# The low part of every eighth weight chunk of the MLPs made by an accumulating DMA

## The chip, the cores and the metric

The kernel runs on one core of one Trainium2 chip. The metric is the device time of one execution in microseconds (us), lower being better, as the median of repeated runs on one chip. Five engines work side by side on the core: TensorE (PE: matmuls, with the weight loads shown apart as PEld), VectorE (DVE), ScalarE (ACT), GpSimd (POOL), which here has had almost nothing to do, and SyncE (SP), which issues the large loads. Transfers from HBM are carried by 16 DMA engines.

## The reference, cut to what matters

The program is a trunk of two layers for 256 tokens of width 2048. Each layer is a mixer (attention and a delta rule in layer 0, dilated attention in layer 1) and an MLP of squared ReLU. Only the MLPs are touched by the change:

```python
D_MODEL, SEQ, DEPTH, D_FF = 2048, 256, 2, 8192

def squared_relu_mlp(h, w1, w2):          # h 256x2048, w1 2048x8192, w2 8192x2048, float32
    return jnp.square(jax.nn.relu(h @ w1)) @ w2

for l in range(DEPTH):
    x = x + mixer_l(rms_norm(x, ...))
    x = x + squared_relu_mlp(rms_norm(x, mlp_norm[l]), mlp_w1[l], mlp_w2[l])
```

## The kernel before, in words

Every large product goes through `dense`. It multiplies 256 tokens (two halves `h` of 128) with a stripe of a weight matrix that is 512 columns wide. The rows of the stripe are taken in chunks `kc` of 128, 16 chunks to a call in the MLPs, so a chunk is a tile of 128x512 float32, 256 KB. Two chunks arrive with one DMA that SP issues (`wload`, 512 KB, the tile whose name ends in `r`; four such buffers).

The product is formed from a high and a low part of each operand. ACT rounds the chunk to the type float32r (line 201, a CAST; tile `...h`, here called the high part). DVE subtracts that from the chunk (line 107 through the helper `tt`; tile `...l`, the low part). The activations were split in the same way earlier. PE then makes three matmuls for each of the two halves: high by high (line 206), high by low part of the weights (line 207), low by high part of the weights (line 208), six for each chunk, all summed in PSUM. High and low parts of the weights have six buffers each, so that ACT and DVE can be at most six chunks ahead of PE; `tc.high_priority(offset=AHEAD)` lets the scheduler place them early.

An MLP runs over four groups `g`. In each group four calls of `dense` make blocks of the hidden layer (names `m_0` to `m_3` in the profile, `b` from 0 to 3), and four calls multiply them with the second matrix (`n_0` to `n_3`). That is 2 layers x 4 groups x 8 calls x 16 chunks = 1024 chunks. After an `m` call ACT applies ReLU and the square (line 123, tiles `m_0r` and so on). `spread` then turns that block for the next product: 16 transposes on DVE (line 289, tile `m_0hT`), a CAST on ACT for its high part (line 314, `m_0hh`) and a subtraction on DVE for its low part (`m_0hl`). These steps are generators; `drip`, called once for each chunk, lets one step of them be recorded in turn, so they stand in ACT's and DVE's queues between the chunks of the next call. Each engine works through its own queue in order, and an instruction that waits holds up all behind it.

In the rows of the program's order below, `m0_0_2l15` is layer 0, group 0, third `m` call, low part of chunk 15; `p0` and `p1` are the sums of the two halves. The profile leaves layer, group and chunk out of a name. Waits name the engine or the DMA semaphore that is waited for.

Of the kernel before, what the change touches and what calls it, by code (L numbers as in the profile page):

```python
# [11 lines left out]
F32 = mybir.dt.float32  # L12
F32R = mybir.dt.float32r
I32 = mybir.dt.int32
AF = mybir.ActivationFunctionType
ALU = mybir.AluOpType
# [3 lines left out]
P = 128  # L20
# [67 lines left out]
def trunk(  # L88
# [5 lines left out]
    V, S, G, E = nc.vector, nc.scalar, nc.gpsimd, nc.tensor  # L94
# [11 lines left out]
    def tt(o, a, b, op):  # L106
        V.tensor_tensor(out=o, in0=a, in1=b, op=op)  # L107
# [13 lines left out]
    def act(o, a, f, scale=1.0, bias=0.0, accum=None):  # L121
        if accum is None:
            S.activation(out=o, in_=a, func=f, scale=scale, bias=bias)  # L123
        else:
            S.activation(out=o, in_=a, func=f, scale=scale, bias=bias, accum_out=accum)
# [45 lines left out]
    def wload(wsrc, k0, nm):  # L171
        raw = wp.tile([P, 2, 512], F32, tag="wr", name=f"{nm}r{k0}", bufs=4)
        off = 0
        for s in wsrc:
            m = s.shape[1]
            nc.sync.dma_start(raw[:, :, off:off + m], s[k0 * P:(k0 + 2) * P, :].rearrange("(c p) n -> p c n", p=P))
            off += m
        return raw
# [3 lines left out]
    def drip():  # L182

        step("gs"[tick[0] % 2])
        if tick[0] % 4 == 3:
            step("o")
        tick[0] += 1

    def dense(wsrc, stat, kcs, nm, pre=(), every=1):

        n = sum(s.shape[1] for s in wsrc)
        ps = [psd.tile([P, 512], F32, tag="d", name=f"{nm}p{h}") for h in range(NH)]
        first, last = kcs[0], kcs[-1]
        for j, kc in enumerate(kcs):
            if j % 2 == 0:
                raw = pre[j // 2] if j // 2 < len(pre) else wload(wsrc, kc, nm)
            w = raw[:, j % 2, :n]
            wh = wp.tile([P, 512], F32R, tag="wh", name=f"{nm}h{kc}")[:, :n]
            wl = wp.tile([P, 512], F32R, tag="wl", name=f"{nm}l{kc}")[:, :n]
            with tc.high_priority(offset=AHEAD):  # L200
                S.copy(wh, w)  # L201
                tt(wl, w, wh.bitcast(F32), ALU.subtract)
            for h in range(NH):
                sh, sl = stat(kc, h)
                o = ps[h][:, :n]
                E.matmul(o, lhsT=sh, rhs=wh, start=kc == first, stop=False)  # L206
                E.matmul(o, lhsT=sh, rhs=wl, start=False, stop=False)  # L207
                E.matmul(o, lhsT=sl, rhs=wh, start=False, stop=kc == last)  # L208
            if j % every == 0:
                drip()  # L210
        return ps
# [91 lines left out]
    def mlp(layer, blocks, hp, done):  # L303
# [15 lines left out]
        for g in range(4):  # L319
            hb = []  # L320
            for b in range(4):
                nm = f"m{layer}_{g}_{b}"
                c0 = (g * 4 + b) * 512
                ps = dense([w1[:, c0:c0 + 512]], stat, KC16, nm)
                r = hp.tile([P, NH, 512], F32, tag="hr", name=nm + "r", bufs=2)
                for h in range(NH):
                    act(r[:, h, :], ps[h], AF.Relu, scale=rstd[:, h:h + 1])
                act(r, r, AF.Square)
                streams["s"].append(spread(r, nm, hb))
            hstat = stat_of(hb)  # L330
            for n in range(4):
                ps = dense([w2[g * 2048:(g + 1) * 2048, n * 512:(n + 1) * 512]], hstat, KC16, f"n{layer}_{g}_{n}")
                add_to_x(n, ps)
                if g == 3:
                    done(n)
# [30 lines left out]
    with ExitStack() as mix:  # L366
# [556 lines left out]
        def do_b(s, pre=()):  # L923
            ps = dense(b_cols(s), xstat, KC16, f"b{s}", pre)
            flush(lambda: "rstd" in ready)
            streams["s"].append(qk_conv(raw_evac(ps, f"b{s}raw"), f"b{s}raw", s, qks))
            streams["g"].append(gdn_of(s))
# [240 lines left out]
```

## Time and profile before

| | |
|---|---|
| median of 3 runs | 2300.85 us (2300.76 to 2300.91) |
| profiled execution | 2301.12 us |
| its span, first to last instruction | 2299.3 us |
| instructions in it | 31489 |
| PE, PEld, DVE, ACT, POOL busy | 2280.7, 1889.1, 1732.9, 1275.7, 5.6 us |
| DMA: packets, moved | 264775, 426.65 MB |
| HBM read, written | 420.11 MB, 4.46 MB |
| mean granted TensorE clock | 0.998 |

Lines of the profile are of one execution, and the sums below are made against its 2301.12 us; that is 0.27 us, or 0.01%, above the median of the runs. Groups of instructions have the form "line engine operation out<-in, shapes xcount | busy us, mean ns of one | idle time of the engine before them and what ended it". In the timeline a row has its start in us, its length, the engine and the operation; "x2" means two instructions merged in one row, and the brackets tell how long the engine had been idle and what ended it. Waits read "engine line <- what it waited for: us in total, times, longest". A table of windows gives the stretch, its length, busy us of each engine with the number of instructions, the granted clock, the busy share of the DMA engines, and GB/s. The chain is the work that ended last, followed back from the end; its pieces read start, us, what, and a DMA's piece runs from its issue to its landing. A matmul's length is modelled and overlaps the next one; the distance between starts is the pace.

### The profile page before, as it was taken

The numbers are of one execution on the slowest core, as the hardware profiler recorded it, in microseconds if no ns is written. First come the engines' busy times: TensorE is split into PE (matmuls) and PEld (weight loads), VectorE is DVE, ScalarE is ACT, GpSimd is POOL, SyncE is SP. The second block draws the span as 40 slices with busy tenths as digits, with TensorE's granted clock in tenths as the row PEclk, the third lists the DMA queues.
The fourth block names the chain that finished last, engine by engine and source line by source line (L and its number), as shares of the span: only waits on it lengthen the run. The fifth ranks groups of instructions, "written<-read, shape, count | busy, mean of one in ns | idle before, by whom it ended". The sixth has DMA issues, their size and how long they took to land.

```text
span 2299.3 us, 31489 instructions
## 1 busy us (share of the span) xinstructions
PE 2280.7 (99%) x10536; PEld 1889.1 (82%) x10536; DVE 1732.9 (75%) x3539; ACT 1275.7 (55%) x2376; POOL 5.6 (0%) x15
## 2 busy tenths in 40 slices
PE   9999999999999999999999999999999999999999
PEld 8888888788888888888888888888888888888887
DVE  6768787867857857857898888987775775775774
ACT  6656756765545545545555565556554554554553
POOL 0000000000000000000000000000000000000000
PEclk9999999999999999999999999999999999999999
DMA  7655464566666666666656555555666666666665
GB/s 251 179 172 167 142 182 140 160 183 182 202 192 183 202 194 188 196 194 189 194 187 201 177 167 174 174 178 177 193 193 193 193 192 193 188 197 194 183 211 163
DMA packets 264775, 426.65 MB, mean 186 GB/s; under 512 B 22514, under 2 KB 94372, under 8 KB 264612
## 3 DMA queue, kind: packets, MB, share of 16 engines
q1 hardware_dynamic: 255812, 420.04, 59.9%
q10 hardware_dynamic: 8800, 4.60, 0.8%
q8 instruction: 82, 1.34, 0.2%
q14 instruction: 81, 0.66, 0.1%
HBM read 420.11 MB, written 4.46 MB: 185 GB/s over the span
## 4 chain that ended last, share of the span: by engine, by line
PE 84%; DVE 10%; ACT 2%; issue 2%; DMA 1%; ACTq 0%; SPq 0%; DVEq 0%
PE m_0p L208 3%; PE m_0p L206 3%; PE m_1p L208 3%; PE m_2p L208 3%; PE n_1p L208 3%; PE n_2p L208 3%; PE m_0p L207 3%; PE n_2p L207 3%; PE n_2p L206 3%; PE n_1p L207 3%; PE m_2p L207 3%; PE m_1p L206 3%; PE m_2p L206 3%; PE n_1p L206 3%; PE m_1p L207 3%; PE n_3p L208 3%
## 5 line engine op out<-in xcount | busy, mean ns | idle before, releaser
L107 DVE TENSOR_TENSOR n_3l<-n_3r,n_3h 128x512 fp32r<-128x512 f32 x128 | 88.3, 691 | 68.3 <-ACT n_3h L201 68.1
L107 DVE TENSOR_TENSOR n_2l<-n_2r,n_2h 128x512 fp32r<-128x512 f32 x128 | 88.2, 691 | 68.3 <-ACT n_2h L201 68.1
L107 DVE TENSOR_TENSOR m_0l<-m_0r,m_0h 128x512 fp32r<-128x512 f32 x128 | 88.4, 691 | 66.3 <-ACT m_0h L201 66.1
L201 ACT CAST n_3h<-n_3r 128x512 fp32r<-128x512 f32 x128 | 79.7, 623 | 89.3 <-DVE n_3l L107 73.6
L201 ACT CAST n_2h<-n_2r 128x512 fp32r<-128x512 f32 x128 | 79.7, 623 | 89.3 <-DVE n_2l L107 73.6
L107 DVE TENSOR_TENSOR n_1l<-n_1r,n_1h 128x512 fp32r<-128x512 f32 x128 | 87.0, 690 | 51.6 <-ACT n_1h L201 51.4
L201 ACT CAST m_0h<-m_0r 128x512 fp32r<-128x512 f32 x128 | 79.7, 623 | 81.8 <-DVE m_0l L107 61.8
L201 ACT CAST n_1h<-n_1r 128x512 fp32r<-128x512 f32 x128 | 78.9, 623 | 77.7 <-DVE n_1l L107 58.1
L201 ACT CAST m_1h<-m_1r 128x512 fp32r<-128x512 f32 x128 | 78.1, 622 | 64.6 <-PE m_1p L208 35.3
L107 DVE TENSOR_TENSOR m_1l<-m_1r,m_1h 128x512 fp32r<-128x512 f32 x128 | 87.1, 691 | 33.7 <-ACT m_1h L201 31.9
L201 ACT CAST m_3h<-m_3r 128x512 fp32r<-128x512 f32 x128 | 77.0, 621 | 47.0 <-PE m_3p L208 35.0
L201 ACT CAST m_2h<-m_2r 128x512 fp32r<-128x512 f32 x128 | 77.0, 621 | 46.8 <-PE m_2p L208 35.3
L201 ACT CAST n_0h<-n_0r 128x512 fp32r<-128x512 f32 x128 | 77.0, 621 | 46.5 <-PE n_0p L208 35.3
L107 DVE TENSOR_TENSOR m_3l<-m_3r,m_3h 128x512 fp32r<-128x512 f32 x128 | 84.9, 689 | 11.6 <-ACT m_3h L201 9.9
L107 DVE TENSOR_TENSOR m_2l<-m_2r,m_2h 128x512 fp32r<-128x512 f32 x128 | 84.9, 690 | 11.2 <-ACT m_2h L201 9.5
L107 DVE TENSOR_TENSOR n_0l<-n_0r,n_0h 128x512 fp32r<-128x512 f32 x128 | 84.9, 689 | 11.0 <-ACT n_0h L201 9.2
L289 DVE STREAM_TRANSPOSE m_0hT<-m_0r 32x256 f32<-32x256 f32 x128 | 55.8, 436 | 10.5 <-ACT m_0r L123 8.0
L289 DVE STREAM_TRANSPOSE m_1hT<-m_1r 32x256 f32<-32x256 f32 x128 | 55.8, 436 | 10.4 <-ACT m_1r L123 7.9
L289 DVE STREAM_TRANSPOSE m_3hT<-m_3r 32x256 f32<-32x256 f32 x128 | 55.8, 436 | 10.4 <-ACT m_3r L123 7.9
L289 DVE STREAM_TRANSPOSE m_2hT<-m_2r 32x256 f32<-32x256 f32 x128 | 55.8, 436 | 10.4 <-ACT m_2r L123 7.9
L208 PE MATMUL n_0p<-n_0h,m_3hl 128*128 128x512 f32 x64 | 25.8, 404 | 1.9 <-DVE m_3hl L107 1.9
L206 PE MATMUL n_0p<-n_0h,m_3hh 128*128 128x512 f32 x64 | 25.0, 390 | 0.0
(2552 smaller groups left out, 7389.0 us busy)
## 6 DMA issues: line engine op xcount, KB each, us to landing
m_0r<-in_mlp_w_dram SPq DMA_DIRECT2D x64, 512.0 KB
m_1r<-in_mlp_w_dram SPq DMA_DIRECT2D x64, 512.0 KB
m_2r<-in_mlp_w_dram SPq DMA_DIRECT2D x64, 512.0 KB
m_3r<-in_mlp_w_dram SPq DMA_DIRECT2D x64, 512.0 KB
n_0r<-in_mlp_w_dram SPq DMA_DIRECT2D x64, 512.0 KB
n_1r<-in_mlp_w_dram SPq DMA_DIRECT2D x64, 512.0 KB
n_2r<-in_mlp_w_dram SPq DMA_DIRECT2D x64, 512.0 KB
n_3r<-in_mlp_w_dram SPq DMA_DIRECT2D x64, 512.0 KB
```

The source lines that it names most:

```text
L107: V.tensor_tensor(out=o, in0=a, in1=b, op=op)
L201: S.copy(wh, w)
L206: E.matmul(o, lhsT=sh, rhs=wh, start=kc == first, stop=False)
L207: E.matmul(o, lhsT=sh, rhs=wl, start=False, stop=False)
L208: E.matmul(o, lhsT=sl, rhs=wh, start=False, stop=kc == last)
L289: V.transpose(out=dv[:, :, :, q], in_=sv[:, :, :, j, :])
```

## The change

In the MLPs (names that begin with `m` or `n`) chunks 7 and 15 of each call, 128 of the 1024, get their low part in another way. ACT writes the rounded negative of the chunk into the low part's buffer with an activation of scale -1 (it is the negated high part). Then POOL issues a DMA that reads the chunk a second time from HBM, 256 KB, and adds it onto that buffer. The subtraction on DVE is dropped for these chunks. The other 896 chunks of the MLPs and all products of the mixers stay as they were.

```diff
             with tc.high_priority(offset=AHEAD):
                 S.copy(wh, w)
-                tt(wl, w, wh.bitcast(F32), ALU.subtract)
+                if nm[0] in "mn" and kc % 8 == 7:
+                    act(wl, w, AF.Identity, scale=-1.0)
+                    G.dma_start(wl, wsrc[0][kc * P:(kc + 1) * P, :].bitcast(F32R), accum_op=ALU.add)
+                else:
+                    tt(wl, w, wh.bitcast(F32), ALU.subtract)
```

Line numbers behind this place grow by four (206 to 210, 289 to 293, 314 to 318). PE's and SP's orders keep their rows, apart from the numbers of buffers and lines. ACT's queue around chunk 15 of an `m` call, before:

```order
L201 CAST m0_0_2h13_6442<-m0_0_2r12_6430 128x512 [waits DVE_49,PE_49]
L314 CAST m0_0_1hh_6404<-m0_0_1hT_6299 128x1024 [waits DVE_49]
L201 CAST m0_0_2h14_6454<-m0_0_2r14_6452 128x512 [waits DMAHW5_49,PE_49,Activation_49]
L201 CAST m0_0_2h15_6464<-m0_0_2r14_6452 128x512 [waits PE_49,Activation_49]
L201 CAST m0_0_3h0_6482<-m0_0_3r0_6480 128x512 [waits DMAHW6_49,PE_49,Activation_49]
L201 CAST m0_0_3h1_6492<-m0_0_3r0_6480 128x512 [waits PE_49,Activation_49]
```

and after the change:

```order
L201 CAST m0_0_2h13_6447<-m0_0_2r12_6435 128x512 [waits PE_49,Activation_49]
L318 CAST m0_0_1hh_6409<-m0_0_1hT_6303 128x1024 [waits DVE_49]
L201 CAST m0_0_2h14_6459<-m0_0_2r14_6457 128x512 [waits DMAHW5_49,PE_49,Activation_49]
L123 ACTIVATE m0_0_2l15_6470<-m0_0_2r14_6457 128x512 [waits DMASW2_49,PE_49]
L201 CAST m0_0_2h15_6469<-m0_0_2r14_6457 128x512 [waits PE_49,Activation_49]
L201 CAST m0_0_3h0_6488<-m0_0_3r0_6486 128x512 [waits DMAHW6_49,PE_49,Activation_49]
L201 CAST m0_0_3h1_6498<-m0_0_3r0_6486 128x512 [waits PE_49,Activation_49]
```

ACT has one more instruction for chunk 15, placed between the CAST of chunk 14 and that of chunk 15, and so still behind the CAST of the previous block's turned tile (`hh`), which waits for DVE.

DVE's queue from chunk 6 of the same call, before:

```order
L107 TENSOR_TENSOR m0_0_2l6_6359<-m0_0_2r6_6356,m0_0_2h6_6358 128x512
L107 TENSOR_TENSOR m0_0_2l7_6369<-m0_0_2r6_6356,m0_0_2h7_6368 128x512
L289 STREAM_TRANSPOSE m0_0_1hT_6299<-m0_0_1r_6271 32x2x4x32 x2
L107 TENSOR_TENSOR m0_0_2l8_6385<-m0_0_2r8_6382,m0_0_2h8_6384 128x512
L289 STREAM_TRANSPOSE m0_0_1hT_6299<-m0_0_1r_6271 32x2x4x32 x3
L107 TENSOR_TENSOR m0_0_2l9_6395<-m0_0_2r8_6382,m0_0_2h9_6394 128x512
L289 STREAM_TRANSPOSE m0_0_1hT_6299<-m0_0_1r_6271 32x2x4x32 x2
L107 TENSOR_TENSOR m0_0_2l10_6411<-m0_0_2r10_6408,m0_0_2h10_6410 128x512
L289 STREAM_TRANSPOSE m0_0_1hT_6299<-m0_0_1r_6271 32x2x4x32 x2
L107 TENSOR_TENSOR m0_0_2l11_6421<-m0_0_2r10_6408,m0_0_2h11_6420 128x512
```

and after:

```order
L107 TENSOR_TENSOR m0_0_2l6_6363<-m0_0_2r6_6360,m0_0_2h6_6362 128x512
L293 STREAM_TRANSPOSE m0_0_1hT_6303<-m0_0_1r_6275 32x2x4x32 x4
L107 TENSOR_TENSOR m0_0_2l8_6390<-m0_0_2r8_6387,m0_0_2h8_6389 128x512
L293 STREAM_TRANSPOSE m0_0_1hT_6303<-m0_0_1r_6275 32x2x4x32 x2
L107 TENSOR_TENSOR m0_0_2l9_6400<-m0_0_2r8_6387,m0_0_2h9_6399 128x512
L293 STREAM_TRANSPOSE m0_0_1hT_6303<-m0_0_1r_6275 32x2x4x32 x3
L107 TENSOR_TENSOR m0_0_2l10_6416<-m0_0_2r10_6413,m0_0_2h10_6415 128x512
L293 STREAM_TRANSPOSE m0_0_1hT_6303<-m0_0_1r_6275 32x2x4x32 x2
L107 TENSOR_TENSOR m0_0_2l11_6426<-m0_0_2r10_6413,m0_0_2h11_6425 128x512
```

The subtraction of chunk 7 is gone, and the transposes that stood behind it move up by its place.

On PE, for the last chunk of that call, before:

```order
L208 MATMUL m0_0_2p1_6276<-m0_0_2h14_6454,xb3l_5879 128x512
L206 MATMUL m0_0_2p0_6275<-m0_0_2h15_6464,xb3h_5878 128x512 [waits Activation_49]
L207 MATMUL m0_0_2p0_6275<-m0_0_2l15_6465,xb3h_5878 128x512 [waits DVE_49]
L208 MATMUL m0_0_2p0_6275<-m0_0_2h15_6464,xb3l_5879 128x512
L206 MATMUL m0_0_2p1_6276<-m0_0_2h15_6464,xb3h_5878 128x512
L207 MATMUL m0_0_2p1_6276<-m0_0_2l15_6465,xb3h_5878 128x512
L208 MATMUL m0_0_2p1_6276<-m0_0_2h15_6464,xb3l_5879 128x512
```

and after:

```order
L212 MATMUL m0_0_2p1_6280<-m0_0_2h14_6459,xb3l_5879 128x512
L210 MATMUL m0_0_2p0_6279<-m0_0_2h15_6469,xb3h_5878 128x512 [waits Activation_49]
L211 MATMUL m0_0_2p0_6279<-m0_0_2l15_6470,xb3h_5878 128x512 [waits DMASW5_49]
L212 MATMUL m0_0_2p0_6279<-m0_0_2h15_6469,xb3l_5879 128x512
L210 MATMUL m0_0_2p1_6280<-m0_0_2h15_6469,xb3h_5878 128x512
L211 MATMUL m0_0_2p1_6280<-m0_0_2l15_6470,xb3h_5878 128x512
L212 MATMUL m0_0_2p1_6280<-m0_0_2h15_6469,xb3l_5879 128x512
```

The order is the same, but the first matmul that reads the low part now waits for a DMA semaphore (DMASW) and no longer for DVE.

POOL's queue, which ended with MEMSETs before, goes on with the 128 DMAs:

```order
L868 MEMSET d3kb_4834 128x1024 [waits PE_49,Activation_49,Pool_49]
L204 DMA m0_0_0l7_5971<-in_mlp_w1_dram 128x512 [waits DVE_49,Activation_49]
L204 DMA m0_0_0l15_6060<-in_mlp_w1_dram 128x512 [waits DVE_49,Activation_49]
L204 DMA m0_0_1l7_6168<-in_mlp_w1_dram 128x512 [waits DVE_49,PE_49,Activation_49]
L204 DMA m0_0_1l15_6265<-in_mlp_w1_dram 128x512 [waits DMASW0_49,DVE_49,Activation_49]
L204 DMA m0_0_2l7_6373<-in_mlp_w1_dram 128x512 [waits DVE_49,DMASW1_49,PE_49,Activation_49]
L204 DMA m0_0_2l15_6470<-in_mlp_w1_dram 128x512 [waits DMASW2_49,DVE_49,Activation_49]
L204 DMA m0_0_3l7_6578<-in_mlp_w1_dram 128x512 [waits DVE_49,DMASW3_49,PE_49,Activation_49]
L204 DMA m0_0_3l15_6675<-in_mlp_w1_dram 128x512 [waits DMASW4_49,DVE_49,Activation_49]
```

Each waits for ACT (the negated part) and for earlier users of its buffer, and nothing else stands between them.

## The prediction

> **What bounds the kernel now.** I read the head of the page first, then the chain and the windows of the two MLPs.
>
> ```profile
> span 2299.3 us, 31489 instructions
> PE 2280.7 (99%) x10536; PEld 1889.1 (82%) x10536; DVE 1732.9 (75%) x3539; ACT 1275.7 (55%) x2376; POOL 5.6 (0%) x15
> ...
> PE 84%; DVE 10%; ACT 2%; issue 2%; DMA 1%; ACTq 0%; SPq 0%; DVEq 0%
> ```
>
> ```profile
> 422.00:1299.00 877.00, 875.93 (x3919) 722.02 (x3918) 660.12 (x1231) 479.76 (x833) 0.00 (x0) 1.00 0.62 191
> 1529.00:2299.00 770.00, 765.66 (x3395) 632.52 (x3393) 542.70 (x918) 401.76 (x659) 0.00 (x0) 1.00 0.63 190
> ```
>
> The second fence holds both MLPs with a little around them: PE is busy for 875.93 of 877 us, at a granted clock of 1.00. A busy PE is not yet a PE at its pace, so the starts of its matmuls come next (timeline, the first chunk of an `n_3` call), beside ACT's CAST of that chunk:
>
> ```profile
> 1014.72 0.39 PE L206 MATMUL n_3p<-n_3h,m_0hh 128*128 128x512 f32 x1
> 1014.94 0.39 PE L207 MATMUL n_3p<-n_3l,m_0hh 128*128 128x512 f32 x1
> 1015.17 0.39 PE L208 MATMUL n_3p<-n_3h,m_0hl 128*128 128x512 f32 x1
> 1015.40 0.39 PE L206 MATMUL n_3p<-n_3h,m_0hh 128*128 128x512 f32 x1
> ...
> 1008.12 0.62 ACT L201 CAST n_3h<-n_3r 128x512 fp32r<-128x512 f32 x1 [0.73 <-DVE n_2l L107]
> ```
>
> Three matmuls take 0.68 us, a chunk of six 1.36 us and a call of 16 chunks 21.76 us. PE is the bound, and ACT and DVE merely have to stay ahead. DVE's 10% of the chain is work followed back past a short wait, not time that PE lost: in the first MLP the waits of PE show one line, 0.9 us in all.
>
> ```profile
> PE n_0p L208 <- DVE m_3hl L107: 0.9, 4, 0.2
> ```
>
> Work taken off DVE can therefore gain next to nothing. What decides is whether the low part made by ACT, POOL and the DMA is there when line 207 wants it. In the rows above ACT ends its CAST at 1008.74 and PE reads the low part at 1014.94. **The lead is 6.20 us**, and it can't grow much, because there are six buffers: five chunks of PE's work (6.8 us) lie between the release of a buffer and its next use, and the CAST takes 0.62 of them.
>
> In the `m` calls ACT and DVE have the previous block to turn as well. The rows of one `m_1` call, chunks 6 and 7, then 14 and 15 (each pair merged into "x2"), with PE's first use of the low parts of 7 and of 15:
>
> ```profile
> 886.04 1.13 ACT L201 CAST m_1h<-m_1r 128x512 fp32r<-128x512 f32 x2
> 893.38 0.39 PE L207 MATMUL m_1p<-m_1l,xb1h 128*128 128x512 f32 x1
> ...
> 898.43 1.05 ACT L314 CAST m_0hh<-m_0hT 128x1024 fp32r<-128x1024 f32 x1 [3.10 <-DVE m_0hT L289]
> 899.39 1.14 ACT L201 CAST m_1h<-m_1r 128x512 fp32r<-128x512 f32 x2
> 904.26 0.39 PE L207 MATMUL m_1p<-m_1l,xb3h 128*128 128x512 f32 x1
> ```
>
> Chunk 7 has 893.38 - 887.17 = 6.2 us. Before chunk 15 ACT sits idle for 3.10 us, waiting for DVE's last transpose, and the lead shrinks to 904.26 - 900.53 = 3.73 us. The `n_0` call carries the same burden, and there PE itself is caught:
>
> ```profile
> 965.46 0.39 PE L207 MATMUL n_0p<-n_0l,m_3hh 128*128 128x512 f32 x1
> 966.07 0.50 PE L208 MATMUL n_0p<-n_0h,m_3hl 128*128 128x512 f32 x1 [0.23 <-DVE m_3hl L107]
> 966.41 0.39 PE L206 MATMUL n_0p<-n_0h,m_3hh 128*128 128x512 f32 x1
> ```
>
> From 965.46 to 966.41 are 0.95 us where two matmuls take 0.45: 0.50 us lost in each of 8 calls, 4.0 us in all.
>
> **The change, part by part.** The engines' work:
>
> ```profile
> L107 DVE TENSOR_TENSOR n_3l<-n_3r,n_3h 128x512 fp32r<-128x512 f32 x128 | 88.3, 691 | 68.3 <-ACT n_3h L201 68.1
> L201 ACT CAST n_3h<-n_3r 128x512 fp32r<-128x512 f32 x128 | 79.7, 623 | 89.3 <-DVE n_3l L107 73.6
> ```
>
> - DVE loses 128 x 0.691 = 88 us, ACT gains 128 activations of the CAST's shape, 128 x 0.62 = 80 us. In the `m_1` call ACT waits 3.10 us in one piece, so two more activations (1.25 us) fit. Neither lies on the path, except at the next point.
> - The subtraction of chunk 7 stood in DVE's queue ahead of the transposes, which therefore end 0.69 + 0.03 = 0.72 us sooner, and with them the wait of `hh`. In `n_0` this exceeds the 0.50 us that PE loses: gain 4.0 us. The lead of chunk 15 becomes 3.73 + 0.72 = 4.45 us, counted from the end of the activation, which takes the place of the old CAST directly behind that of chunk 14. In `n_0` it is about the same. The high part comes one activation later, with over 2 us to spare.
> - Chunk 7 of these calls has its activation behind its CAST: 6.20 - 0.62 = 5.58 us. In `m_0` and in `n_1` to `n_3` the activation stands ahead of the CAST: about 6.4 us, as its buffer comes free one matmul (0.23) sooner.
> - SP's queue is as before; a pair of chunks in the load buffer is free no later, since ACT reads the last one where DVE did. In POOL's queue only the next accumulating DMA stands behind a waiting one, and that is 8 chunks (10.9 us) later.
> - Behind line 207's wait stands all of PE. A delay is paid in full, 128 times if it is everywhere: buffers tie ACT to PE again after each stall, so no reserve is built up.
>
> The unknown is L, from the end of ACT's activation to the landing. No accumulating DMA and no DMA of POOL is in the trace. The nearest rows are, from the chain, a small store by ACT's queue (16x128, 8 KB) and a 512-KB load, and from the page the queue of the loads (packets, MB, share):
>
> ```profile
> 75.10 2.52 DMA scg<-grow_t
> 129.73 4.10 DMA av0r<-in_ab_w_in_dram
> q1 hardware_dynamic: 255812, 420.04, 59.9%
> ```
>
> Low end 2.5 us (the store, as if the bytes cost nothing); high end 8.2 us (twice the load, as if the data went out and back in turn). My value starts from the load. The last row gives 0.599 x 16 x 2299.3 / 255812 = 86 ns for a packet; 512 KB in rows of 2 KB are 16 for each of 16 engines, 1.4 us, which leaves 2.7 us fixed. The new DMA has 8 rows per engine, but reads HBM, reads the buffer and writes it: 8 x 3 x 86 ns = 2.1 us if these don't overlap. I add 0.6 us, an estimate of about a CAST's length, for POOL to make up the transfer and for meeting a weight load (DMA share 0.62). **L = 2.7 + 2.1 + 0.6 = 5.4 us.**
>
> The Trainium skill ("DMA: Bandwidth & Descriptors", section "Anatomy of one DMA — SWDGE (gpsimd) path") fits a POOL-issued DMA with about 2.0 us plus bytes over 436 GB/s. By it 256 KB take 2.6 us, 3.2 us if the buffer's reading counts as bytes too; no row here can test it, as it gives nothing for an accumulation. Then no chunk is late, which is the first rival.
>
> The sum, where lateness is L minus the lead:
> - chunk 15 of `m_1` to `m_3` (24), of `n_0` (8), and three like them where the next norm is turned: 35 x (5.4 - 4.45) = 33 us
> - chunk 7 of `m_1` to `m_3` and `n_0` (32, lead 5.58): 0
> - the remaining 61 (lead about 6.4): 0
> - `n_0`'s wait gone: -4 us
>
> Together +29 us on 2301.1, so **2330 us**, 1.3% slower (0.3 us less against the median). At L = 6.0 it is 35 x 1.55 - 4 = +50 (a delay at chunk 7 is taken off that of chunk 15, since DVE runs on meanwhile), at 7.0 35 x 2.55 + 61 x 0.6 - 4 = +122, at 8.2 about +260.
>
> The skill has a rule that speaks against the change ("SBUF — State Buffer", section "Who interferes with whom"): POOL can't write the descriptors of its DMA while DVE runs in a two-port mode, which it allows to copies and tensor_scalar, not to tensor_tensor. The MLPs' DVE rows are TENSOR_TENSOR and STREAM_TRANSPOSE, so by the rule nothing is added; if DVE did block POOL for one instruction, L would be 6.1 and the sum +54.
>
> **The rivals.**
> 1. Not slower: L is below 4.45 us. For it: the load with twice the bytes took 4.10. Against it: an accumulation touches the bytes three times, through a queue that this kernel never used. The time is 2301 - 4 = 2297 us. It decides at L = 4.57, where 35 x 0.12 eats the 4 us; up to 4.70 the loss stays below 4.6 us, 0.2% of the time, which is what a measurement of this kernel can tell from no change.
> 2. All 128 chunks late: L over 6.4, for instance because the engines add slowly. 35 x 1.95 - 4 = +64 us at 6.4, +122 at 7.0, +260 at 8.2: 2365 to 2560 us.
> 3. The second read starves the weight loads. In a call 8 loads are 128 packets per engine and two accumulations 48 packet times: a share of 0.62 x 176/128 = 0.85, still below 1. It decides from five packet times for a row of the accumulation (1.01); at six (1.085) the 64 calls of 21.76 us would stretch by 8.5%, 118 us, to 2419. Below that, an ordinary chunk's CAST may come 5 us late before PE notices (6.20 less the subtraction).
> 4. Faster by over 0.2%: beyond the 4 us in `n_0` PE has nothing to give in the MLPs, so its pace of 0.227 us would have to improve, for which no row speaks.
>
> **How the numbers follow.** L between 4.70 and 6.4 (the forecast): 0.46; rival 1: 0.25; rival 2: 0.21; rival 3: 0.03; rival 4: 0.05. Range from 2296 (rival 1) to 2420 (L = 7.0), which leaves out the upper part of rival 2 and rival 4, about 0.15 together. The forecast's own range is 2306 to 2365. Faster 0.05, same 0.25, slower 0.70.
>
> **What would show it.** Right: PE waits at line 211 for DMAs onto `m_1l`, `m_2l`, `m_3l`, `n_0l`, about 1 us each, some 35 times, and none in `n_1` to `n_3`; DVE busy about 1645 us, ACT about 1356; the wait of `n_0p` for `m_3hl` gone; a new queue with 33.6 MB. Wrong: no such waits (L was shorter), waits at all 128 (longer), or waits of ACT for `m_0r` and its like (loads starved).

## The result, and the profile after

The changed kernel takes 2395.44 us (median; 2391.01 to 2399.94), the kernel before on the same chip 2300.88 us: ratio 1.0412, 95% interval 1.0399 to 1.0424, or +94.6 us where +29 was forecast. The sign and the mechanism were as forecast, the size was over three times as large. The profiled execution is one of the slower ones, with a span 98.9 us longer than before. Its head, its chain and the windows of both MLPs, the same stretches as before apart from their length:

```profile
span 2398.2 us, 31999 instructions
PE 2314.9 (97%) x10536; PEld 1883.2 (79%) x10536; DVE 1665.4 (69%) x3411; ACT 1342.9 (56%) x2504; POOL 116.2 (5%) x143
...
q0 software_dynamic: 18432, 33.56, 8.3%
...
PE 50%; issue 25%; DMA 13%; DVE 8%; ACT 2%; POOL 2%; ACTq 0%; SPq 0%; POOLq 0%; DVEq 0%
```

```profile
422.00:1349.00 927.00, 894.72 (x3930) 720.89 (x3929) 629.52 (x1170) 514.55 (x900) 55.41 (x64) 1.00 0.70 199
1579.00:2396.00 817.00, 780.78 (x3378) 627.31 (x3376) 504.95 (x847) 434.36 (x720) 55.26 (x64) 1.00 0.70 199
```

The first MLP grew from 877 to 927 us and the second from 770 to 817: all of the loss lies there. PE is now idle for 32 and 36 us in these stretches, and a DMA stands in the chain with 13%. Whom PE waits for (us in total, times, longest):

```profile
PE m_1p L211 <- DMA m_1l<-in_mlp_w_dram: 13.8, 11, 2.7
PE n_0p L211 <- DMA n_0l<-in_mlp_w_dram: 12.8, 12, 1.9
PE m_2p L211 <- DMA m_2l<-in_mlp_w_dram: 10.2, 8, 2.1
PE m_3p L211 <- DMA m_3l<-in_mlp_w_dram: 9.9, 9, 1.4
PE n_1p L211 <- DMA n_1l<-in_mlp_w_dram: 4.8, 9, 2.2
PE n_2p L211 <- DMA n_2l<-in_mlp_w_dram: 4.7, 10, 1.5
PE m_0p L211 <- DMA m_0l<-in_mlp_w_dram: 4.5, 6, 1.1
PE n_3p L211 <- DMA n_3l<-in_mlp_w_dram: 4.1, 11, 0.7
```

The wait of `n_0p` for `m_3hl` is gone, as forecast; the eight new ones add up to 64.8 us. This table counts a wait only from the modelled end of the matmul before it; counted from start to start, against the pace of 0.2267 us, PE loses 103.0 us in the MLPs where it lost 3.9 before, and the 99.1 us between them account for the whole difference. One late chunk, from the chain (chunk 15 of the first `m_1` call; start, us, what):

```profile
549.01 0.54 ACT m_1l L123
549.56 0.28 issue
549.84 5.45 DMA m_1l<-in_mlp_w_dram
555.29 0.04 issue
555.34 0.50 PE m_1p L211
```

From ACT's end (549.56) to the landing (555.29) are 5.73 us, the L of the prediction, and PE resumes 0.05 us later. The view of the DMAs gives the stretch from POOL's issue to the landing (median us, last column):

```profile
m_1l<-in_mlp_w_dram POOLq DMA_DIRECT2D x16, 256.0 KB, 5.6
m_2l<-in_mlp_w_dram POOLq DMA_DIRECT2D x16, 256.0 KB, 5.5
...
n_2l<-in_mlp_w_dram POOLq DMA_DIRECT2D x16, 256.0 KB, 6.5
n_3l<-in_mlp_w_dram POOLq DMA_DIRECT2D x16, 256.0 KB, 6.5
```

With the 0.29 us before POOL's issue these are L = 5.8 to 6.8, not 5.4. For each of the 128 chunks I took from the trace ACT's end, the landing and the start of line 211. A chunk counts as late if PE starts within 0.05 us of the landing. "Lead" is the time from ACT's end to line 211 in a run in which nearly nothing is late (the chip-source run below).

| chunks | number | lead, forecast | lead, measured | L, mean (forecast 5.4) | late | PE's pause, sum us |
|---|---|---|---|---|---|---|
| 15 of `m_1`-`m_3` | 24 | 4.45 | 4.29 | 6.13 | 24 | 36.2 |
| 15 of `n_0` | 8 | 4.45 | 4.31 | 6.32 | 8 | 12.3 |
| 7 of `m_1`-`m_3` | 24 | 5.58 | 5.56 | 5.74 | 19 | 3.9 |
| 7 of `n_0` | 8 | 5.58 | 5.52 | 5.99 | 8 | 3.2 |
| both of `m_0` | 16 | 6.4 | 6.4-6.5 | 6.4 and 6.9 | 9 | 5.9 |
| both of `n_1`-`n_3` | 48 | 6.4 | 6.1 | 6.6-6.7 | 44 | 21.0 |

So the pauses at line 211 come to 82.3 us over 112 late chunks. Another 12.9 us are lost at the matmul right behind them (about 0.1 us for each pause; the late matmul's own row above reads 0.50 us where others read 0.39). The remaining 8 us are small delays in the matmuls after that; the granted clock fell to half for 3.4 us three times here, which is most of them (3 x 1.7 us). The 4.2 us of `n_0` are gained. At chunk 15 the pauses are shorter than L less the lead of the table (36.2 us where 24 x 1.84 would be 44), which fits the prediction's remark that a delay at chunk 7 is taken off that of chunk 15 (chunk 7 with the matmul behind it loses 6 us in these calls).

### The profile page after: what moved, and what is told of

It reads as the page before. It is cut to its first block, busy times and chain, and to the rows that moved or that the text cites. A ratio compares the mean times of both kernels' runs of the same rounds, so it can differ in the third digit from the quotient of the medians.

```text
span 2398.2 us, 31999 instructions
## 1 busy us (share of the span) xinstructions
PE 2314.9 (97%) x10536; PEld 1883.2 (79%) x10536; DVE 1665.4 (69%) x3411; ACT 1342.9 (56%) x2504; POOL 116.2 (5%) x143
## 4 chain that ended last, share of the span: by engine, by line
PE 50%; issue 25%; DMA 13%; DVE 8%; ACT 2%; POOL 2%; ACTq 0%; SPq 0%; POOLq 0%; DVEq 0%
DMA m_1l<-in_mlp_w_dram 3%; DMA m_2l<-in_mlp_w_dram 2%; DMA m_3l<-in_mlp_w_dram 2%; PE m_2p L211 2%; PE m_3p L211 2%; PE m_0p L211 2%; PE m_2p L212 2%; PE m_3p L212 2%; PE m_2p L210 2%; PE m_0p L212 2%; PE m_3p L210 2%; DMA m_0l<-in_mlp_w_dram 2%; PE m_0p L210 2%; PE m_1p L211 2%; PE m_1p L212 1%
## 5 line engine op out<-in xcount | busy, mean ns | idle before, releaser
L107 DVE TENSOR_TENSOR n_3l<-n_3r,n_3h 128x512 fp32r<-128x512 f32 x112 | 77.5, 692 | 86.6 <-ACT n_3h L201 86.3
L107 DVE TENSOR_TENSOR n_2l<-n_2r,n_2h 128x512 fp32r<-128x512 f32 x112 | 77.5, 692 | 85.2 <-ACT n_2h L201 85.0
L107 DVE TENSOR_TENSOR m_0l<-m_0r,m_0h 128x512 fp32r<-128x512 f32 x112 | 77.4, 692 | 81.4 <-ACT m_0h L201 81.0
L107 DVE TENSOR_TENSOR n_1l<-n_1r,n_1h 128x512 fp32r<-128x512 f32 x112 | 77.0, 692 | 65.4 <-ACT n_1h L201 64.8
L107 DVE TENSOR_TENSOR m_1l<-m_1r,m_1h 128x512 fp32r<-128x512 f32 x112 | 77.5, 692 | 46.7 <-ACT m_1h L201 44.9
L107 DVE TENSOR_TENSOR m_2l<-m_2r,m_2h 128x512 fp32r<-128x512 f32 x112 | 76.8, 692 | 38.1 <-ACT m_2h L201 36.3
L107 DVE TENSOR_TENSOR m_3l<-m_3r,m_3h 128x512 fp32r<-128x512 f32 x112 | 76.9, 692 | 36.0 <-ACT m_3h L201 34.1
L107 DVE TENSOR_TENSOR n_0l<-n_0r,n_0h 128x512 fp32r<-128x512 f32 x112 | 76.7, 691 | 33.3 <-ACT n_0h L201 31.2
L204 POOL DMA_DIRECT2D m_0l<-in_mlp_w_dram x16 | 13.9, 872 | 660.9 <-DVE xd3eq L107 395.4
L211 PE MATMUL n_0p<-n_0l,m_3hh 128*128 128x512 f32 x64 | 25.8, 404 | 11.0 <-DMA n_0l<-in_mlp_w_dram 11.0
```

What stands on the lines that cost most here:

```text
L204: G.dma_start(wl, wsrc[0][kc * P:(kc + 1) * P, :].bitcast(F32R), accum_op=ALU.add)
```

## The experiments

My theory: the cost is L minus the lead, chunk by chunk, and L is long because of what goes on beside the DMA. The rivals: L is long because the addition itself is slow; the second read of HBM costs; the loads are starved; or the removal and the activations cost something on the engines.

**The DMA left out.** Edit: the line `G.dma_start(...)` deleted.

> The 128 accumulating DMAs are left out; ACT still writes the negated high part, and PE multiplies with that, so the low part of those 128 chunks is wrong. Both theories of the late landing: PE waits for none of them and the 4 us that the call n_0 lost before are gone, 2296.7 us. The rival that ACT's added 80 us or the new order of DVE cost something of their own: above 2301 us.

Measured: 2296.22 us, ratio 0.9983 (0.9974 to 0.9993). The waits of PE for `m_1l` and its like are gone, and the windows read

```profile
422.00:1299.00 877.00, 876.87 (x3927) 724.24 (x3928) 624.35 (x1166) 513.80 (x899) 0.00 (x0) 1.00 0.62 191
```

ACT's extra 34 us in the first MLP (513.80 against 479.76) cost nothing, and the 4 us are really there: all of the loss comes with the DMA.

**One of the two chunks alone.** Edit: `kc % 8 == 7` becomes `kc == 7`, or `kc == 15`.

> Only chunk 7 takes the new way; chunk 15 has DVE's subtraction back. By the leads: chunk 7's 26.8 us stay, n_0's gain of 4.2 us stays, chunk 15's 72.7 us go: 2323 us (2316 to 2330). By an equal cost for every accumulating DMA: 2348 us.

Measured: 2323.92 us, ratio 1.0104 (1.0091 to 1.0118). The lead accounts for it to within 1 us, an equal price for each DMA does not.

> Only chunk 15 of each MLP product takes the new way; chunk 7 has DVE's subtraction back (64 accumulating DMAs instead of 128). If the cost is chunk 15's lateness (landing after the lead), chunk 7's 26.8 us go, n_0 gets back its wait of 4.2 us, and chunk 15's lead in m_1 to m_3 and n_0 falls by the 0.7 us that chunk 7 had freed on DVE, 32 chunks by 0.7 = 23 us at the most: 2373 to 2396 us. If instead every accumulating DMA costs the same (94.5 us over 128), 64 of them cost 47 us: 2348 us.

Measured: 2457.18 us, ratio 1.0682 (1.0665 to 1.0698). Half as many DMAs cost 62 us more than all of them, and 61 us more than the upper end of what I expected:

```profile
PE m_3p L211 <- DMA m_3l<-in_mlp_w_dram: 25.9, 8, 4.1
PE m_1p L211 <- DMA m_1l<-in_mlp_w_dram: 25.3, 8, 3.5
PE m_2p L211 <- DMA m_2l<-in_mlp_w_dram: 22.1, 8, 3.3
PE n_0p L211 <- DMA n_0l<-in_mlp_w_dram: 22.1, 8, 4.0
```

The pauses at chunk 15 of `m_1` to `m_3` rose from 36.2 to 77.3 us, those of `n_0` from 12.3 to 23.4. Two reasons were not in my sum. First, ACT's queue now has both CASTs of the pair ahead of the activation, so the activation is the last reader of the load buffer, and SP's next load starts 0.06 us after POOL's issue instead of 0.58 (rows of POOL and SP, changed kernel first, then this one):

```profile
549.84 0.86 POOL L204 DMA_DIRECT2D m_1l<-in_mlp_w_dram  x1 [11.46 <-ACT m_1l L123]
550.42 0.37 SPq L176 DMA_DIRECT2D m_2r<-in_mlp_w_dram  x1
```

```profile
550.91 0.87 POOL L204 DMA_DIRECT2D m_1l<-in_mlp_w_dram  x1 [24.58 <-PE m_1p L212]
550.96 0.37 SPq L176 DMA_DIRECT2D m_2r<-in_mlp_w_dram  x1
```

L rose with it from 6.13 to 6.54 us. The lead fell to 3.4 us: from ACT's end to line 211 are 6.59 us, 3.22 of them pause. Second, the granted clock: 22 dips to half in this profile (next to three), 78.5 us in all, worth up to 39 us at half the pace. The first of them, in windows:

```profile
540.00:556.00 16.00, 13.84 (x62) 11.12 (x60) 13.31 (x24) 7.92 (x13) 0.87 (x1) 1.00 0.64 173
...
557.00:563.00 6.00, 5.83 (x14) 4.57 (x15) 1.56 (x3) 3.57 (x5) 0.00 (x0) 0.50 0.38 117
```

In 6 us PE starts 14 matmuls instead of 26. So chunk 7's subtraction, taken away, does more for chunk 15 than the 0.72 us that the prediction put down for it.

**A plain copy instead of the addition.** Edit: `accum_op=ALU.add` dropped.

> The DMA copies the chunk instead of adding it, so the low part of the 128 chunks is the whole chunk. Theory of contention (the DMA is late because it meets weight loads on the same 16 engines): a packet falls from 178 to about 90 ns, landing comes 8 x 0.09 = 0.7 us sooner and the rest of the delay stays, about 2340 us. Theory of the addition (adding is what is slow): the delay is gone, 2297 to 2301 us.

Measured: 2358.97 us, ratio 1.0256 (1.0236 to 1.0277). POOL's instruction takes 528 ns where it took 863, the queue's share is 5.6% where it was 8.3%, and L is shorter by 0.6 to 1.5 us, except at chunk 15 of `n_0` (first POOL's row among the groups by line, then the page's row of the queue, then the DMAs, which stood at 5.6 and 6.5):

```profile
L204 POOL DMA_DIRECT2D m_1l<-in_mlp_w_dram x16 | 8.4, 528 | 180.3 <-ACT m_1l L123 93.8 <-PE m_1p L212 75.5 <-DVE m_1l L107 11.1
```

```profile
q0 software_dynamic: 18432, 33.56, 5.6%
```

```profile
m_1l<-in_mlp_w_dram POOLq DMA_DIRECT2D x16, 256.0 KB, 5.3
...
n_2l<-in_mlp_w_dram POOLq DMA_DIRECT2D x16, 256.0 KB, 5.1
```

In the trace's packet records a packet of 2 KB takes 99 ns (median), the accumulating one 178 ns. Eight per engine make 0.63 us, POOL 0.34 us: the addition is worth about 1 us of L and 36 of the 94.6 us. The shorter instruction also changes an order: where SP's load is issued 0.24 us after POOL's DMA, the first plain packet starts 1.2 to 1.5 us after POOL's issue, the first accumulating one 2.6 to 3.1 (means of the groups of `m_0` and `n_1` to `n_3`). The time is 19 us above what the theory of contention gave and far above what that of the addition gave: the addition is a part, not the cause.

**No weight loads beside it.** Edit: the MLPs load the first eight chunks of each layer and use them again.

```diff
-                raw = pre[j // 2] if j // 2 < len(pre) else wload(wsrc, kc, nm)
+                if nm[0] in "mn":
+                    if len(fixed) < 4:
+                        fixed.append(wload(wsrc, kc, nm))
+                    raw = fixed[(j // 2) % 4]
+                else:
+                    raw = pre[j // 2] if j // 2 < len(pre) else wload(wsrc, kc, nm)
...
+        fixed.clear()
```

> The MLPs load only their first eight chunks in each layer and use them for all calls; the accumulating DMAs stay, so the results of the MLPs are wrong. No weight load of SP runs beside the 128 DMAs, but for the first few. Theory of contention: from ACT's end to the landing 0.29 + 1.57 + 8 x 0.178 + 0.35 = 3.6 us, less than the shortest lead, so 2296.7 us. Theory of the addition: still about 6 us from ACT's end to the landing, at least 2380 us.

Measured: 2310.78 us, ratio 1.0048 (1.0033 to 1.0063). The DMAs, from issue to landing:

```profile
m_1l<-in_mlp_w_dram POOLq DMA_DIRECT2D x16, 256.0 KB, 4.2
...
n_2l<-in_mlp_w_dram POOLq DMA_DIRECT2D x16, 256.0 KB, 4.1
```

Without loads the groups' L is 4.3 to 4.8 us. That takes away most of the loss, but L did not fall to the 3.6 us that I had added up from its parts (from the first packet's start to the last one's end it takes 2.2 to 2.4 us, not 8 x 0.178 = 1.4), so chunk 15, with its lead of 4.3 us, is still late by about 0.25 us in 32 calls.

**The chunk read out of the load buffer.** Edit: `G.dma_start(wl, w.bitcast(F32R), accum_op=ALU.add)`.

> The DMA adds the chunk from its load buffer on the chip instead of reading it a second time from HBM; the sum is the same. Theory of contention, where the time goes in the queues of the 16 engines: 2380 to 2410 us as with the change. Theory that the second read from HBM is what is slow: at least 30 us less, below 2365 us.

Measured: 2297.82 us, ratio 0.9992 (0.9982 to 1.0003). 5 chunks of 128 are late, and the loss is gone (DMAs from issue to landing):

```profile
m_1l<-m_1r POOLq DMA_DIRECT2D x16, 256.0 KB, 3.2
...
n_2l<-n_2r POOLq DMA_DIRECT2D x16, 256.0 KB, 4.2
```

By its time alone the theory of the second read would be right and that of contention wrong, but the edit changes two things: HBM is not read again, and the DMA now reads the load buffer, so SP's next load waits for the landing. It starts 3.56 us after POOL's issue (timeline of POOL and of SP):

```profile
549.54 0.86 POOL L204 DMA_DIRECT2D m_1l<-m_1r  x1 [11.45 <-DVE m_0hl L107]
553.10 1.39 SPq L176 DMA_DIRECT2D m_2r<-in_mlp_w_dram  x3
```

**The two parted.** First the source on the chip with the load not held (a fixed tile of zeros as the source):

```diff
-                    G.dma_start(wl, wsrc[0][kc * P:(kc + 1) * P, :].bitcast(F32R), accum_op=ALU.add)
+                    G.dma_start(wl, low[-1].bitcast(F32R), accum_op=ALU.add)
...
+        fx = hp.tile([P, 512], F32, name="fx", bufs=1)
+        V.memset(fx, 0.0)
+        low.append(fx)
```

> The DMA adds a fixed tile of zeros that lies on the chip, so the low part of the 128 chunks stays the negated high part. Unlike the run that added the chunk from its load buffer, nothing holds that buffer, so SP issues the next weight load 0.2 to 0.6 us behind POOL's DMA, as with the change. Theory of the load (the weight load issued beside the DMA makes it late): again 5.5 us or more from ACT's end to the landing, above 2340 us. Theory of the second read (reading HBM makes it late): 3.6 to 4.4 us, 2296 to 2302 us.

Measured: 2377.56 us, ratio 1.0345 (1.0329 to 1.0360), and 102 chunks are late, for the DMA is no faster than in the changed kernel:

```profile
m_1l<-fx POOLq DMA_DIRECT2D x16, 256.0 KB, 5.3
...
n_2l<-fx POOLq DMA_DIRECT2D x16, 256.0 KB, 6.6
```

Then the source in HBM with the load held, by a one-column addition on POOL behind the DMA that reads the landed tile and the load buffer:

```diff
+                    G.tensor_tensor(out=low[-1], in0=wl[:, :1].bitcast(F32), in1=w[:, :1], op=ALU.add)
...
+        low.append(hp.tile([P, 1], F32, name="dm", bufs=1))
```

> The DMA reads HBM as with the change, but a one-column operation on POOL reads its result and the load buffer, so that SP can issue the next weight load into that buffer only after the landing. Theory of the load: about the 4.5 us of the run without loads, 2297 to 2315 us. Theory of the second read: still 6 us, above 2360 us.

Measured: 2341.87 us, ratio 1.0190 (1.0173 to 1.0207), between the two expectations. A part of it was my edit's: in the `n` calls all matmuls were slow. I ran it again with the column in a tile of 2 KB per partition:

> As the run that held the load buffer by a one-column addition on POOL with the source in HBM, but the column lies in a tile of 2 KB per partition instead of one of 4 bytes, since there the matmuls of the n products alone ran at 0.2333 us instead of 0.2267 us, 20.5 us in all. If the 4-byte tile, which shifts the tiles behind it, was the reason, the pace is 0.2267 again and the time 2341.9 - 20.5 = 2321 us; the load beside the DMA is then worth 2395 - 2321 = 74 of the 94.5 us. If holding the loads itself slows TensorE, it stays at 2342 us.

Measured: 2336.07 us, ratio 1.0157 (1.0143 to 1.0171). The matmul rows (by line), first with the 4-byte tile, then with the 2-KB tile:

```profile
L212 PE MATMUL n_2p<-n_2h,m_0hh 128*128 128x512 f32 x64 | 25.3, 396 | 0.0
```

```profile
L212 PE MATMUL n_2p<-n_2h,m_0hh 128*128 128x512 f32 x64 | 24.9, 389 | 0.0
```

The pace is 0.2267 us again, so the small tile was the reason, yet the time fell by 6 us, not 21: where PE had been held back by its own pace, it now waits for the landing instead (pauses at chunks 7 and 15 rose from 27 to 40 us, counted as excess over the pace). Here are the landings:

```profile
m_1l<-in_mlp_w_dram POOLq DMA_DIRECT2D x16, 256.0 KB, 4.4
...
n_2l<-in_mlp_w_dram POOLq DMA_DIRECT2D x16, 256.0 KB, 4.6
```

Together four kernels make a square (median less that of the kernel before on the same chip, in us, and the group means of L):

| | next load beside the DMA | next load held until the landing |
|---|---|---|
| source in HBM | +94.6 (L 5.7 to 6.9) | +36.0 (L 4.5 to 5.0) |
| source on the chip | +78.9 (L 5.4 to 6.9) | -2.1 (L 3.5 to 4.5) |

Holding the load is worth 59 to 81 us, the source 16 to 38 us. The load beside the DMA is the main cause; the longer way from HBM decides most of what is left, because the lead of chunk 15 is 4.3 us and its L without the load lies on one side of it (3.8 from the chip) or on the other (4.8 to 4.9 from HBM). Holding has a price of its own, though, so the +36.0 are not the source's alone: ACT's CASTs now wait 93 us for the later loads (39 us with the chip source, 1.3 us in the kernel before), and ten chunks of `n_1` to `n_3`, six of them with an L of 6.2 us or more, paused for 10.8 us. The largest of these waits of ACT:

```profile
ACT n_1h L202 <- DMA n_1r<-in_mlp_w_dram: 29.4, 15, 2.9
```

**More lead.** Edit: the low parts in question get two buffers of their own, and ACT's activation and the DMA are placed four to five chunks earlier.

> The low parts made by DMA get two buffers of their own, so ACT's activation no longer waits for one of the six and stands four to five chunks earlier, ahead of the wait for the transposes. The DMA is the change's own, from HBM. All theories: the lead becomes 10 us or more, every landing is in time, and 2296.7 us is reached; if the lateness were not a matter of lead (a fixed cost at each DMA, such as PE's resuming), it would stay above 2350 us.

Measured: 2407.52 us, ratio 1.0477 (1.0461 to 1.0492). No wait for a low part's DMA is left, since the landings come 0.7 us or more before use, in the median 4.0. But ACT now reaches the activation before the chunk itself has arrived:

```profile
ACT n_3l L123 <- DMA n_3r<-in_mlp_w_dram: 91.0, 16, 7.2
ACT n_2l L123 <- DMA n_2r<-in_mlp_w_dram: 87.6, 16, 7.1
...
PE n_0p L215 <- ACT m_3hh L324: 10.5, 8, 1.8
```

ACT takes its queue in order, so all CASTs behind it wait too, and PE loses 112 us, nearly all of it at chunks 2 and 3 and 10 to 14. The wait moved from PE's queue into ACT's. With the source on the chip it is the same in kind:

> Both repairs: the chunk is added from its load buffer, and the low part has its own two buffers, so the result is the full one without a second read of HBM. 2296.5 us, 0.15 to 0.19% under the kernel before. If holding the load buffers until the landing delays weight loads, ACT waits for loads and the time is above 2300 us.

Measured: 2359.92 us, ratio 1.0273 (1.0258 to 1.0288), ACT waiting 60.7 us for `m_2r` and 32 to 60 us for each of `n_1r`, `m_3r`, `n_0r`, `n_3r`, `n_2r` and `m_0r`.

**What the square points to.** Source on the chip, and chunk 7 alone, whose lead is 5.5 us and more.

> Only chunk 7 takes the new way, and the accumulating DMA reads the chunk out of the load buffer on the chip, not out of HBM. The landing comes 3.5 to 4.5 us after ACT's end there, chunk 7's lead is 5.6 us or more, so nothing is late and the 4.2 us of n_0 are gained without the 1.7 us that chunk 15 cost with the same source: 2296.5 us (ratio 0.998). Rival: holding the load buffer makes the next weight load late, and the time is not under 2300 us.

Measured: 2295.32 us, ratio 0.9979 (0.9970 to 0.9988). PE waits for no low part, as the landing comes 0.6 us or more before its use, in the median 2.2. From POOL's issue to the landing (rows of the tiles `m_1l`, then `n_2l`; 8 DMAs each):

```profile
DMA to landing us min/median/max: 3.2/3.2/3.2
```

```profile
DMA to landing us min/median/max: 3.2/3.4/4.2
```

It is the fastest of all versions, 0.2% ahead of the kernel before; by its interval it can't be told from the run without a DMA, which is the floor of this idea.

## Why the prediction was wrong in size

- **The bound, the leads, the sign: right.** The forecast leads of 4.45, 5.58 and 6.4 us were measured as 4.3, 5.5 and 6.1 to 6.5. DVE's busy time fell by 67 us (88 forecast) and ACT's rose by 67 (80), neither of which the time shows; `n_0` gained its 4 us, and the rest is lateness at line 211, paid in full.
- **The failed step is the term L = 2.7 + 2.1 + 0.6 = 5.4 us**, the last 0.6 us of it above all, "for POOL to make up the transfer and for meeting a weight load". L measured 5.7 to 6.9, with a mean of 6.3 over the 128 chunks. A DMA that is alone needs 4.3 to 4.8 us from HBM (no-loads run) and 3.5 to 4.5 us from the chip with the next load held, so the first two terms, 4.8 together, were about right in sum. That was partly luck, for the parts differ: 0.29 us from ACT's end to POOL's issue, 1.6 to the first packet and 0.3 from the last one to the landing make 2.2 us fixed, not 2.7, with POOL's making up of the transfer inside them, and a packet takes 178 ns, not 258, but from the first one's start to the last one's end are 2.2 to 2.4 us from HBM, not 8 x 0.178 = 1.4.
- **The third term, 0.6 us, is the one that was mis-sized.** What I took for a meeting by chance, priced by a mean share of 0.62, is a meeting by design: ACT's last readings of the pair of chunks, of which the activation is one, also free the load buffer, so in 124 of the 128 cases a 512-KB load of SP is issued between 0.3 us before POOL's DMA and 0.6 us after it, and takes the same engines. Against the run with the load held that is 1.2 to 2.1 us more in every group of chunks, where I had put 0.6.
- **"The remaining 61: 0"** fell with it: an L of 6.4 to 6.9 exceeded leads of 6.1 to 6.5, and these chunks paid 26.9 us; chunk 7 of `m_1` to `n_0`, forecast at 0 too, paid 7.1. 112 chunks were late, which is rival 2, to which I gave 0.21; the time lies inside my outer range (2296 to 2420) and outside the forecast's own (2306 to 2365). The ground of rival 2, slow adding, is worth 36 us; the load beside it is worth more.
- **L alone doesn't close the sum.** With L = 6.3 my own sum gives 35 x 1.85 - 4 = +61 us. In the profiled execution chunk 15 of `m_1` to `m_3` and of `n_0` cost 48.4 us, the chunks that I had put at nothing (with the three where the next norm is turned) 34, and what follows a pause 21. Two smaller slips: at L = 8.2 my formula gives 35 x 3.75 + 61 x 1.8 - 4 = +237 and not +260, and at L = 4.70 the loss is 4.75 us, not below 4.6.
- **A pause costs more than its length.** The 12.9 us at the following matmuls and the 8 us behind them, clock dips above all, were not in the sum.
- **Rival 1** needs L below 4.57: it came true only with source and load both changed. **Rival 3** did not come: an ordinary chunk's CAST waits for no load in the changed kernel. **Rival 4** was right in its bound: nothing beats the kernel before by more than about 5 us.
- Nothing shows DVE holding POOL up: POOL's accumulating instruction took 0.86 to 0.89 us (means by tile) in every run that has it, and without loads L was 4.3 to 4.8 us beside the same kinds of DVE operations. The Trainium skill's rule on DVE's two-port modes ("SBUF — State Buffer", section "Who interferes with whom") was itself not tried, as DVE's operations in the MLPs are TENSOR_TENSOR and STREAM_TRANSPOSE in all runs. The Trainium skill's fit for a POOL-issued DMA ("DMA: Bandwidth & Descriptors", section "Anatomy of one DMA — SWDGE (gpsimd) path") gave 3.2 us if the buffer's reading counts as bytes; the undisturbed accumulation from the chip, 3.2 us from issue to landing in its fastest groups, agrees, that from HBM, 4.0 to 4.2 us, does not.

What stays open: why pauses add about 0.1 us at the next matmul, why an undisturbed accumulation from HBM spreads its packets over 2.2 to 2.4 us and one from the chip over as little as 1.5, and which other versions of the order of loads and accumulations would keep them apart at no price.

## What to carry to other kernels

Price a new DMA by its distance to the nearest use, chunk by chunk, and ask which other transfer the same event releases: a mean share of the DMA engines says nothing about a load that starts in the same half microsecond every time. Six buffers gave a fixed lead here, and moving the producer forward with buffers of its own only made it wait for its own input, with all behind it in its queue. If an accumulating DMA must be, let it read what is already on the chip and hold the load buffer until it has landed.

## What the runs showed of the hardware

- An accumulating packet of 2 KB takes 178 ns where a plain one takes 99; POOL's instruction for it 863 ns where the plain one takes 528.
- A load issued from 0.3 us before POOL's issue to 0.24 us after it moves the first accumulating packet from 1.6 us after the issue to 2.6 to 3.1 (means of the groups in the changed kernel); one issued 0.58 us after it leaves the first packet at 1.6 and spreads the packets over 3.9 to 4.1 us, where they take 2.6 with the load held.
- Within each run the granted clock falls to half on a fixed raster of 3.41 us, for one such window (once for two in a row). PE's lost time in each window, start to start against the pace, summed over the MLPs of the two kernels and all twelve experiments, parts them cleanly: each of the 40 windows at full clock that lost 2.03 us or more was followed by a dip, and none of the 5818 that lost 2.01 us or less. So a dip goes with the idle time inside one window, not with the length of a pause: in the chunk-15 run 7 of the 19 pauses of over 3 us passed without a dip, and in the run with the earlier activation, where no pause reached 2 us, several in one window brought five. The Trainium skill ("TensorE: Matmul & The Clock Gate", section "Why this matters for your kernels") tells to avoid idle gaps above about 3 us; here shorter ones were enough.
- A tile of 4 bytes per partition, ahead of the stationary operands of the `n` calls (`hh`, `hl`) in their pool, slowed the matmuls of these calls from 0.2267 to 0.2333 us; with a tile of 2 KB in its place the pace was 0.2267 again.
